# Attention's output projection per 256 rows by seven block products in place of eight

## The chip, the cores and the metric

The kernel runs on one core of a Trainium2 chip, in one launch. The core has a matrix engine (TensorE, PE in the profile, with its weight loads as PEld), three engines for work on elements (VectorE or DVE, ScalarE or ACT, GpSimd or POOL), and queues for transfers between DRAM and the on-chip memory (SBUF); matrix results land in eight banks of a second memory (PSUM). Each engine executes its own list in the order in which it was written down, and waits for the others through semaphores. The metric is the device time of one execution in microseconds (us): the median of some runs.

## The reference

One encoder layer is applied to two sequences of 1024 rows and 1024 columns, in fp32. Beside attention there is a Fourier mixing, which is not touched. What matters here:

```python
q = (rmsnorm(q_lat, g_q_lat) @ w_uq).reshape(b, s, MLA_HEADS, QK_DIM)      # 4 heads
...
p = jax.nn.softmax(sc, axis=-1)
o = einsum('bhqk,bkhd->bqhd', p, v)                                        # width 4 * 128 = 512
mix = jnp.concatenate([y_mla, y_four], axis=-1) @ w_out                    # the output projection
x = x + ga1 * mix                                                          # gate per sequence
h2 = rmsnorm(x, g_ffn) * (1.0 + sc2) + sh2
ffn = (silu(h2 @ w_gate) * (h2 @ w_up)) @ w_down
return x + ga2 * ffn
```

The kernel multiplies `w_out` with the values' up-projection ahead of time, so that each head's output is taken straight in the latent space of 128 columns: per sequence the attention half of the output projection is a product of (1024 rows x 512) with a (512 x 1024) matrix `wv`, which also carries the gate `ga1`.

## The kernel before

**Numbers.** Every fp32 product is made from pieces. A value is split into a high part, rounded to the type fp32r, and the rest (`split`, lines 62 to 64: a copy on ScalarE, a subtraction on VectorE), and `mm3` (lines 78 to 81) adds high x high, high x low and low x high in one bank. So each 128 x 512 piece of a product with 128 rows in the contraction is three matmuls, whose lines in the profile are 79, 80 and 81.

**Stages.** Input projections; the Fourier mixing (`p2`); attention (`p3`, with the output projection and the norm behind it, `p4`); the feed-forward (`p5`), which already works with seven products in place of eight on 512 x 512 blocks. The Fourier result and the input x are added in DRAM in `fo_d`; `out_load` fetches 128 of its rows into a tile `x2`, the output projection adds to it, `norm2` stores it, squares it and scales it, and `flip_h` transposes it for the feed-forward.

**Attention's loop.** Line 1499 runs k over 64 items, sequence s by block b of 256 rows by head h by half block u of 128 rows, and four steps more. Step k issues, in this order: `scores` of item k (10 matmuls, maximum on VectorE, exponential on ScalarE, scaling on VectorE), queries of the next block (`rope_q`, `rope_flip`, `absorb_q`), after each second head `values` of the pair (24 matmuls into one bank, j = 0 or 1), the transposes and splits of item k-1 (`flip_p`), then with m = k - 10 the output of the block that is a block and two steps behind (`out_step`), and what `todo[k]` has (weights, loads, additions of x). `out_proj` makes 128 rows x 512 columns of one block from 4 heads x 3 = 12 matmuls, in steps 0, 2, 4 and 6 of eight, in a bank of the pair `g`, which queries and `values` use too; one addition on VectorE takes it to `x2`. `wv` is loaded, gated on POOL (`wv_gate`) and split (`wv_split`) for sequence 0 in steps 5 to 13 and for sequence 1 in steps 37 to 43.

**Order.** A planner writes each engine's list: of what is ready by its own estimate of durations, what comes first in the program goes first. `tc.issue_after(x)` keeps instructions behind x on x's engine, `behind()` behind the last split, and `first(early, late)` keeps an order of two instructions. A tile with `bufs=n` has n buffers; a new one waits for the release of the one n before. Pools opened after others were closed use their bytes, and wait tile by tile.

**The seam.** Steps 64 to 67 issue `out_proj` of block (1,2), the last transposes and the last `values`. Then the pools of the feed-forward are opened. `prep_h` loads and splits seven prepared blocks `H` of sequence 0 (staging tiles H20, H21, H30, H31; two pieces for each `next(prep)`), `sums_w` makes the first weight combinations on VectorE, `out_proj` of block (1,3) follows in four pieces, with `norm3`, `flip2` (16 transposes of block (1,2)) and more of `prep_h` between; the feed-forward's weight chunk is split by `hl`. The first chunk (n = 0) uses one H per product and splits the others on the way; the second chunk's weight sums are made on VectorE in it.

## Time and profile before

| | |
|---|---|
| time, median of 3 runs | 1994.22 us (1994.19 to 1996.29) |
| the profiled execution | 1991.72 us, its span 1989.9 us |
| TensorE busy | 1965.3 us (99%), 9554 matmuls |
| VectorE, ScalarE, POOL busy | 1382.5 (69%), 893.7 (45%), 831.0 (42%) us |
| granted TensorE clock | 0.998 |
| attention, first scores to last | 278.3 to 682.0 us |
| matmuls of the output projection | 384, from 331.2 to 714.3 us |

The profile shows one execution, so its durations add up to its own time, 1991.72 us, which is 2.5 us below the median. Busy time of an engine is the time in which it executed anything; matmuls overlap each other, so the step from one start to the next is shorter than one duration.

### The profile page before, as it was taken

To read this page: it belongs to the slowest core of one execution; us is meant where nothing else is said; L and a number is where in the kernel's file an instruction comes from. 1 tells how busy PE (TensorE), PEld (TensorE's weight loads), DVE (VectorE), ACT (ScalarE), POOL (GpSimd) and SP (SyncE) were. 2 spreads that over 40 slices of the span, in tenths; PEclk is the share of its full clock that TensorE was granted. 3 is DMA by queue.
4 is the path that set the end of the run, shared out by engine and by line. 5 is a ranking of instruction groups with operands and counts; after the bars stand their busy time and mean duration, and the time that the engine had idled before them with its cause. 6 is when DMAs were issued, how large, how long until landed. Compare 5 with 4: busy or idle time off the path is not lost.

```text
span 1989.9 us, 27639 instructions
## 1 busy us (share of the span) xinstructions
PE 1965.3 (99%) x9554; PEld 1621.7 (81%) x9554; DVE 1382.5 (69%) x2081; ACT 893.7 (45%) x1743; POOL 831.0 (42%) x1008
## 2 busy tenths in 40 slices
PE   8999999999999999999999999999999999999998
PEld 6788778888888878888888888888888888888886
DVE  5667767666777687877767668779655665656794
ACT  5764545555565563333333355443333333335551
POOL 2554012111312348977877401345644544510152
PEclk9999999999999999999999999999999999999999
DMA  9986965535354584654655597774322322357762
GB/s 392 333 318 227 358 237 116 110 91 160 101 117 138 191 283 166 218 181 172 200 182 190 171 316 231 239 230 150 133 96 90 132 94 92 116 199 241 254 228 85
DMA packets 167081, 377.12 MB, mean 190 GB/s; under 512 B 18044, under 2 KB 43260, under 8 KB 163740
## 3 DMA queue, kind: packets, MB, share of 16 engines
q1 hardware_dynamic: 144252, 304.03, 45.2%
q0 software_dynamic: 22112, 70.27, 11.4%
q8 instruction: 75, 1.23, 0.2%
q10 hardware_dynamic: 576, 1.05, 0.1%
q14 instruction: 66, 0.54, 0.1%
HBM read 263.01 MB, written 120.65 MB: 193 GB/s over the span
## 4 chain that ended last, share of the span: by engine, by line
PE 59%; DVE 2%; issue 1%; POOL 1%; DMA 1%; ACT 0%; SPq 0%; POOLq 0%; DVEq 0%; ACTq 0%
PE bank L80 20%; PE bank L79 20%; PE bank L81 20%; DVE wl L64 1%; DMA draw<-in_w_down_dram 1%; DVE val L1987 0%; DVE val L154 0%; DVE val L1878 0%; DVE H L64 0%; DMA val<-x_d 0%; POOL rs_y L107 0%; POOL val L154 0%; DVE val L151 0%; POOL out_dram L1993 0%; DVE val L1875 0%
## 5 line engine op out<-in xcount | busy, mean ns | idle before, releaser
L79 PE MATMUL bank<-H,wh 128*128 128x512 f32 x1232 | 480.2, 390 | 2.6 <-DVE val L154 0.9
L80 PE MATMUL bank<-H,wh 128*128 128x512 f32 x1232 | 479.5, 389 | 0.3 <-DVE H L64 0.3
L81 PE MATMUL bank<-H,wl 128*128 128x512 f32 x1232 | 479.3, 389 | 0.2 <-DVE wl L64 0.2
L79 PEld LDWEIGHTS bank<-H,wh 128*128 128x128 f32 x1232 | 231.2, 188 | 53.2 <-DVE val L1861 2.0
L64 DVE TENSOR_TENSOR wl<-draw,wh 128x512 fp32r<-128x512 f32 x286 | 209.0, 768 | 94.0 <-ACT wh L63 93.5
L81 PEld LDWEIGHTS bank<-H,wl 128*128 128x128 f32 x1232 | 231.3, 188 | 49.0 <-DVE wl L64 0.5
L80 PEld LDWEIGHTS bank<-H,wh 128*128 128x128 f32 x1232 | 231.3, 188 | 48.2 <-DVE H L64 0.6
L154 DVE TENSOR_TENSOR val<-bank,val 128x512 f32<-128x512 f32 x200 | 136.6, 689 | 163.0 <-PE bank L81 162.1
L63 ACT CAST wh<-draw 128x512 fp32r<-128x512 f32 x286 | 164.9, 619 | 173.2 <-PE bank L80 131.6
L154 POOL TENSOR_TENSOR val<-val 128x512 f32<-128x512 f32 x58 | 82.4, 1421 | 345.7 <-DVE val L1959 163.5
L80 PE MATMUL bank<-wl,wh 128*128 128x512 f32 x572 | 223.2, 390 | 0.8 <-DVE wl L64 0.5
L63 ACT CAST wh<-rgu 128x512 fp32r<-128x512 f32 x172 | 107.1, 623 | 258.4 <-PE bank L80 203.2
L81 PE MATMUL bank<-wh,wl 128*128 128x512 f32 x572 | 222.6, 389 | 0.0
L79 PE MATMUL bank<-wh 128*128 128x512 f32 x572 | 222.6, 389 | 0.0
L63 ACT CAST wh<-val 128x512 fp32r<-128x512 f32 x133 | 82.3, 622 | 261.9 <-PE bank L80 249.3
L64 DVE TENSOR_TENSOR wl<-val,wh 128x512 fp32r<-128x512 f32 x133 | 126.1, 950 | 65.4 <-ACT wh L63 65.3
L64 DVE TENSOR_TENSOR wl<-rgu,wh 128x512 fp32r<-128x512 f32 x172 | 162.5, 945 | 0.8 <-ACT wh L63 0.7
L151 POOL TENSOR_TENSOR val<-rgu 128x512 f32<-128x512 f32 x80 | 108.3, 1354 | 78.7 <-DMA rgu<-in_wgu_dram 74.9
L80 PEld LDWEIGHTS bank<-wl,wh 128*128 128x128 f32 x572 | 107.4, 188 | 25.2 <-DVE wl L64 2.9
L79 PEld LDWEIGHTS bank<-wh 128*128 128x128 f32 x572 | 107.4, 188 | 22.5
L81 PEld LDWEIGHTS bank<-wh,wl 128*128 128x128 f32 x572 | 107.4, 188 | 21.9
L151 POOL TENSOR_TENSOR val<-val 128x512 f32<-128x512 f32 x89 | 119.1, 1356 | 1.3
(403 smaller groups left out, 3885.5 us busy)
## 6 DMA issues: line engine op xcount, KB each, us to landing
rgu<-in_wgu_dram SPq DMA_DIRECT2D x86, 512.0 KB, 4.0
draw<-s_d SPq DMA_DIRECT2D x143, 256.0 KB, 3.4
s_d<-val POOLq DMA_DIRECT2D x88, 256.0 KB, 3.0
draw<-t_d SPq DMA_DIRECT2D x88, 256.0 KB, 4.2
s_d<-val SPq DMA_DIRECT2D x66, 256.0 KB, 3.8
draw<-in_w_down_dram SPq DMA_DIRECT2D x55, 256.0 KB, 4.1
xt<-in_x_dram SPq DMA_DIRECT2D x16, 512.0 KB, 7.3
wada<-in_w_ada_dram SPq DMA_DIRECT2D x16, 512.0 KB, 9.8
```

The costliest lines, as they stand in the source:

```text
L63: here["a"] = nc.scalar.copy(hi, src).ins
L64: here["v"] = (eng or nc.vector).tensor_tensor(out=lo, in0=src, in1=rd(hi), op=ALU.subtract).ins
L79: nc.tensor.matmul(out, lh, rh, start=first, stop=False, skip_group_check=cont)
L80: nc.tensor.matmul(out, lh, rl, start=False, stop=False, skip_group_check=cont)
L81: here["t"] = here["pe"] = nc.tensor.matmul(out, ll, rh, start=False, stop=last, skip_group_check=cont).ins
L151: return eng.tensor_tensor(out=out, in0=x, in1=y, op=ALU.subtract).ins
L154: eng.tensor_tensor(out=out, in0=x, in1=y, op=ALU.add)
```

## The change

A block of 256 rows x 512 (the heads' outputs, transposed) times 512 x 1024 is cut in halves along all three axes: rows u, heads 0-1 and 2-3, columns g. Seven products of 128 rows x 256 x 512 columns, each 2 chunks x 3 matmuls, take the place of eight. With A the left operand and B the weights, they are m1 = A11 B11, m2 = A12 B21, m3 = S4 B22, m4 = A22 (B21 - T2), m5 = S1 T1, m6 = S2 T2, m7 = S3 (B22 - B12), where S1 = A21 + A22, S2 = S1 - A11, S3 = A11 - A21, S4 = A12 - S2, T1 = B12 - B11 and T2 = B22 - T1. The results are C11 = m1 + m2, C21 = m1 + m6 + m7 + m4, C22 = m1 + m6 + m7 + m5, C12 = m1 + m6 + m5 + m3.

The left operands are made when `values` is done, the weights once per sequence (`wv_sum` on POOL, seven products' weights split in `wv_split`). One product is issued per step, in the order of `PROD`; the sum m1 + m6 goes to three places by additions on POOL. Row half 1 is complete after m4, row half 0 after m3, so `norm2` and `flip_h` take them in that order. The first four products of block (1,2) are issued in steps 58 to 61 in place of after the loop. The tiles for this take 18 KB per partition more in `p4`; four tags get one buffer less each, H60 and H61 go to a pool that opens after `p4` is closed, and the row tile `x3` is dropped. The functions `sub` and `add` that are called are one tensor_tensor each on the engine named (lines 151 and 154).

```diff
     def half(name):
-        return e.tile([P, 512], F32, tag="hv", name=name, bufs=2)
+        return e.tile([P, 512], F32, tag="hv", name=name, bufs=1)
...
-        qp = e.tile([P, HEADS, P], F32R, tag="qp", name="qp", bufs=4)
+        qp = e.tile([P, HEADS, P], F32R, tag="qp", name="qp", bufs=3)
...
-        qa = [e.tile([P, 256], F32R, tag=f"qa{i}", name=f"qa{i}", bufs=3) for i in range(2)]
+        qa = [e.tile([P, 256], F32R, tag=f"qa{i}", name=f"qa{i}", bufs=2) for i in range(2)]
         split(qa[0], qa[1], pq[:, :256])
         S["qa", s, b, h] = qa
...
-    wv = [tl.tile([P, HEADS, D], F32R, tag=f"wv{i}", name=f"wv{i}") for i in range(2)]
+    wv = [tl.tile([P, 7, 2, 512], F32R, tag=f"wv{i}", name=f"wv{i}") for i in range(2)]
...
-    def out_proj(s, b, u, g):
-        o, x2 = S["o", s, b], S["x2", s, b, u]
-        us = slice(u * P, u * P + P)
-        gs = slice(512 * g, 512 * g + 512)
+    PROD = ("m1", "m7", "m6", "m5", "m4", "m2", "m3")
+    WEIGHT = {"m1": 0, "m2": 1, "m3": 2, "m5": 3, "m6": 4, "m7": 5, "m4": 6}
+
+    def part(name, bufs=1):
+        return [tl.tile([P, 2, P], F32R, tag=f"{name}{i}", name=f"{name}{i}", bufs=bufs) for i in range(2)]
+
+    def rest(name):
+        return tl.tile([P, 2, P], F32, tag=name, name=name, bufs=1)
+
+    def low(t, src, eng):
+        here["a"] = nc.scalar.copy(t[0], src).ins
+        eng.tensor_tensor(out=t[1], in0=src, in1=rd(t[0]), op=ALU.subtract)
+
+    def left_half(s, b, po):
+        f = S["f", s, b] = {"a21": rest("fa"), "s3": rest("fs")}
+        o = S["o", s, b] = {"m1": part("oa")}
+        nc.scalar.copy(f["a21"], po[:, :, 1, :])
+        split(*o["m1"], po[:, :, 0, :])
+        sub(f["s3"], po[:, :, 0, :], f["a21"], nc.vector)
+
+    def right_half(s, b, po):
+        f, o = S["f", s, b], S["o", s, b]
+        for k, u in (("m2", 0), ("m4", 1)):
+            o[k] = part(("ob", "oc")[u])
+            split(*o[k], po[:, :, u, :])
+        s2, s4 = rest("ft"), rest("fu")
+        sub(s2, po[:, :, 1, :], f["s3"], nc.vector)
+        add(f["a21"], f["a21"], po[:, :, 1, :], nc.vector)
+        sub(s4, po[:, :, 0, :], s2, nc.vector)
+        for k, v in (("m6", s2), ("m5", f["a21"]), ("m3", s4)):
+            o[k] = part(f"o{k}")
+            low(o[k], v, nc.gpsimd)
+
+    def out_proj(s, b, i):
+        k = PROD[i]
+        o, x = S["o", s, b], [S.get(("x2", s, b, u)) for u in range(2)]
+        lh, ll = o.pop(k)
+        wi = WEIGHT[k]
         pm = gbank()
-        for h in range(HEADS):
-            mm3(pm, o[0][:, h, us], o[1][:, h, us], wv[0][:, h, gs], wv[1][:, h, gs], h == 0, h == HEADS - 1)
-        here["v"] = nc.vector.tensor_tensor(out=x2[:, gs], in0=x2[:, gs], in1=pm, op=ALU.add).ins
+        for c in range(2):
+            mm3(pm, lh[:, c, :], ll[:, c, :], wv[0][:, wi, c, :], wv[1][:, wi, c, :], c == 0, c == 1)
+        if k == "m1":
+            S["u"] = tl.tile([P, 512], F32, tag="u", name="u", bufs=1)
+            nc.scalar.copy(S["u"], pm)
+            o["m7"] = part("oa")
+            low(o["m7"], S.pop(("f", s, b))["s3"], nc.gpsimd)
+
+        def to(u, g, v, eng=None):
+            t = x[u][:, 512 * g : 512 * g + 512]
+            here["v" if eng is None else "p"] = (eng or nc.vector).tensor_tensor(out=t, in0=t, in1=v, op=ALU.add).ins
+
+        for u, g in {"m1": ((0, 0),), "m7": ((1, 0), (1, 1)), "m5": ((1, 1), (0, 1)), "m4": ((1, 0),), "m2": ((0, 0),),
+                     "m3": ((0, 1),)}.get(k, ()):
+            to(u, g, pm)
+        if k == "m6":
+            here["v"] = nc.vector.tensor_tensor(out=S["u"], in0=S["u"], in1=pm, op=ALU.add).ins
+            for u, g in ((1, 0), (1, 1), (0, 1)):
+                to(u, g, S["u"], nc.gpsimd)
...
-        if i % 2 == 0:
-            out_proj(s, b, i // 4, i // 2 % 2)
-        if i in (2, 6):
-            norm2(s, b, i // 4, tl)
-        if i == 4:
-            flip_h(s, b, 0)
+        if i < 7:
+            out_proj(s, b, i)
+        if i in (4, 6):
+            norm2(s, b, 3 - i // 2, tl)
+        if i == 6:
+            flip_h(s, b, 1)
...
-            p = w.tile([P, N], F32, tag="p", name="p", bufs=3)
+            p = w.tile([P, N], F32, tag="p", name="p", bufs=2)
...
-            if j == 0:
-                S["o", s, b] = [tl.tile([P, HEADS, 256], F32R, tag=f"o{i}", name=f"o{i}b{s}{b}", bufs=3) for i in range(2)]
-            o = S["o", s, b]
             po = gbank()
             for c in range(8):
                 mm3(po, ckv[:, c, 0, :], ckv[:, c, 1, :], pth[:, c], ptl[:, c], c == 0, c == 7)
-            split(o[0][:, 2 * j : 2 * j + 2, :], o[1][:, 2 * j : 2 * j + 2, :], po.rearrange("p (h q) -> p h q", h=2))
+            (left_half, right_half)[j](s, b, po.rearrange("p (h u q) -> p h u q", h=2, u=2))
...
-        def wv_split(i):
-            h, g = i % 4, i // 4
-            gs = slice(512 * g, 512 * g + 512)
-            with behind():
-                split(wv[0][:, h, gs], wv[1][:, h, gs], S.pop(("wv", h, g)))
+        def wv_split(k, blk):
+            wi = WEIGHT[k]
+            for c in range(2):
+                with behind():
+                    split(wv[0][:, wi, c, :], wv[1][:, wi, c, :], S["wv", 2 * (blk // 2) + c, blk % 2])
+
+        def wv_sum(out, x, y):
+            for c in range(2):
+                o, x_, y_ = (S["wv", 2 * (blk // 2) + c, blk % 2] for blk in (out, x, y))
+                with tc.issue_after(here["p"]):
+                    here["p"] = sub(o, x_, y_, nc.gpsimd)
...
+        for q, k0 in enumerate((4, 36)):
+            for i in range(8):
+                todo[k0 + i // 4].append(lambda i=i: wv_gate(i))
+                if i == 3:
+                    todo[k0].append(lambda q=q: gate_half(q, 1))
+            for d, k, blk, sums in ((2, "m1", 0, ((0, 1, 0), (1, 3, 1))), (4, "m7", 1, ()), (4, "m3", 3, ((3, 3, 0),)),
+                                    (5, "m6", 3, ()), (6, "m5", 0, ()), (6, "m2", 2, ((2, 2, 3),)), (7, "m4", 2, ())):
+                todo[k0 + d].append(lambda k=k, blk=blk: wv_split(k, blk))
+                for out, x, y in sums:
+                    todo[k0 + d].append(lambda out=out, x=x, y=y: wv_sum(out, x, y))
...
-            todo[60 + u].append(lambda u=u: out_load(1, 2, u))
+            todo[57].append(lambda u=u: out_load(1, 2, u))
...
+                if k == nit:
+                    out_proj(1, 2, 4)
+                    norm2(1, 2, 1, tl)
+                    for i in (5, 6):
+                        out_proj(1, 2, i)
+                    S["tail", 3] = here["v"]
...
+            if 48 <= m < 52:
+                out_proj(1, 2, m - 48)
...
-            return w.tile([P, 4, 512], dt, tag=tag, name=tag, bufs=1)
+            return (S["w6"] if tag[:2] == "H6" else w).tile([P, 4, 512], dt, tag=tag, name=tag, bufs=1)
...
-                x2 = tl.tile([P, D], F32, tag="o0", name="x3", bufs=3) if u == 0 else xn
+                x2 = xn
...
-            first(here["a"], S.pop(("tail", 5)))
-            first(here["v"], S.pop(("tail", 6)))
-            first(here["v"], S.pop(("tail", 2)))
-            first(here["v"], S["tail", 4])
-            first(here["a"], S.pop(("tail", 7)))
...
-        norm2(1, 2, 1, xb)
+        norm2(1, 2, 0, xb)
...
-        for n in range(4):
-            out_proj(1, 3, n // 2, n % 2)
-            if n == 1:
-                norm3(0)()
-            prep_step((2, 0, 0, 0)[n])
-            if n == 1:
+        for n in range(7):
+            out_proj(1, 3, n)
+            if n == 4:
...
+        S["w6"] = st.enter_context(tc.tile_pool(name="p5c", bufs=1, reuse_waits="tile"))
+        for i in range(2):
+            quad(f"H6{i}")
...
-                            S["n3"] = norm3(1, S.pop("jk3").bitcast(BF16))
+                            S["n3"] = norm3(0, S.pop("jk3").bitcast(BF16))
```

28 lines of the change are left out of this document (8 added, 20 removed).

## The prediction

> **What bounds the kernel now.** I read the page's first part, then the groups of matmuls, then stretches of the span, and last the timeline where attention ends.
>
> ```profile
> span 1989.9 us, 27639 instructions
> ## 1 busy us (share of the span) xinstructions
> PE 1965.3 (99%) x9554; PEld 1621.7 (81%) x9554; DVE 1382.5 (69%) x2081; ACT 893.7 (45%) x1743; POOL 831.0 (42%) x1008
> ```
>
> TensorE (PE) is busy for 99% of the span, and only 24.6 us are without a matmul. Work that leaves TensorE shortens the kernel, unless another engine then sets the pace. The groups touched are these (instructions | busy, mean ns of one):
>
> ```profile
> L79 PE MATMUL gb<-wv,o0b 128*128 128x512 f32 x128 | 52.3, 408 | 0.0
> L81 PE MATMUL gb<-wv,o1b 128*128 128x512 f32 x128 | 51.0, 399 | 0.0
> L80 PE MATMUL gb<-wv,o0b 128*128 128x512 f32 x128 | 50.7, 396 | 0.0
> ```
>
> 384 matmuls belong to the output projection: 8 blocks of 256 rows, 4 pieces each, 12 matmuls a piece. Their 400 ns aren't the price, since matmuls overlap. The price is the step from start to start, read from the timeline of TensorE:
>
> ```profile
> 682.00 0.39 PE L1399 MATMUL ps_s<-lat,qp 128*128 128x512 f32 x1
> ...
> 689.70 0.39 PE L79 MATMUL gb<-pt,ckv 128*128 128x512 f32 x1
> ...
> 705.82 0.39 PE L81 MATMUL gb<-wv,o1b 128*128 128x512 f32 x1
> ...
> 714.55 0.39 PE L79 MATMUL bank<-H,wh 128*128 128x512 f32 x1
> ```
>
> From 689.70 to 705.82 TensorE starts 72 matmuls without a break (24 of the last `values`, 48 of `out_proj`): 16.12 us / 71 = 0.227 us each. The same rows give the landmarks of the seam: the last scores at 682.00, the last `values` from 689.70, the feed-forward's first product at 714.55. The stretches (length, then PE, PEld, DVE, ACT and POOL busy):
>
> ```profile
> 690.50:714.50 24.00, 23.18 (x110) 18.75 (x109) 15.46 (x20) 12.71 (x21) 7.78 (x21) 1.00 0.78 283
> 714.50:735.00 20.50, 18.37 (x84) 14.00 (x83) 20.30 (x26) 16.18 (x23) 8.15 (x9) 1.00 0.71 246
> 284.00:682.00 398.00, 395.28 (x2178) 333.74 (x2177) 285.94 (x526) 224.84 (x457) 96.84 (x154) 1.00 0.47 126
> ```
>
> In attention (284 to 682) TensorE lacks only 2.7 us of 398, and VectorE (DVE) is busy 72%: TensorE sets the pace. In the first 20.5 us of the feed-forward it is the other way round: VectorE is busy 20.30 of 20.50 us, TensorE 18.37. The chain that ended last says the same, for between these two pieces all its named work is VectorE's:
>
> ```profile
> 720.72 1.21 DVE wl L64 x2
> ...
> 735.01 0.50 PE bank L79
> ```
>
> **What the change removes.** A block has 7 products of 2 chunks x 3 matmuls = 42 matmuls instead of 48. Over 8 blocks that is 48 fewer, 48 x 0.227 = 10.9 us. That is the most the change can give. How much of it stays depends on where the matmuls go. Now six blocks (288 matmuls) lie ahead of 682.00 and 96 behind. The loop of the changed kernel issues the first four products of block (1,2) in steps 58 to 61, so 6 x 42 + 24 = 276 lie ahead and 60 behind. Ahead of the last scores 12 x 0.227 = **2.7 us** are saved; behind them TensorE has 36 x 0.227 = 8.2 us less to do.
>
> **What it adds.** The prices (groups of one stretch of attention, and one pair of steps of VectorE):
>
> ```profile
> L1343 DVE TENSOR_TENSOR x<-x,gb 128x512 f32<-128x512 f32 x18 | 12.2, 679 | 1.6 <-PE gb L81 1.6
> L1468 POOL TENSOR_TENSOR wvr<-wvr,gah 128x512 f32<-128x512 f32 x8 | 11.8, 1510 | 0.0
> ...
> L64 DVE TENSOR_TENSOR qa<-gb,qa 128x256 fp32r<-128x256 f32 x18 | 7.5, 416 | 0.6 <-ACT qa L63 0.6
> ...
> L64 DVE TENSOR_TENSOR o1b<-gb,o0b 128x512 fp32r<-128x512 f32 x9 | 6.2, 693 | 18.3 <-ACT o0b L63 18.3
> L1023 POOL TENSOR_TENSOR qt<-qt 128x256 f32<-128x256 f32 x8 | 5.9, 736 | 36.8 <-DVE qt L1022 36.8
> ...
> L63 ACT CAST qa<-gb 128x256 fp32r<-128x256 f32 x18 | 6.7, 372 | 17.0 <-PE gb L81 17.0
> ```
>
> ```profile
> 713.93 1.51 DVE L1343 TENSOR_TENSOR xn<-xn,gb 128x512 f32<-128x512 f32 x2
> 715.35 0.69 DVE L64 TENSOR_TENSOR wl<-rgu,wh 128x512 fp32r<-128x512 f32 x1
> 715.96 0.69 DVE L64 TENSOR_TENSOR wl<-H,wh 128x512 fp32r<-128x512 f32 x1
> ```
>
> Instructions of VectorE overlap a little: 0.69 us of duration is a step of 0.61 us (715.35 to 715.96), so I count 0.61 for 512 columns and, with the same 0.08 off, 0.34 for 256.
>
> Per block, VectorE: `left_half` has two 256-column operations and `right_half` five, in place of two 512-column splits: 7 x 0.34 - 2 x 0.61 = +1.2. The products bring nine 512-column additions instead of four: +3.1. Together **+4.3 us** of VectorE per block. ScalarE: eight operations of 256 columns (0.37 each) and one copy of 512, instead of two casts of 512, +2.4 us. GpSimd (POOL): four subtractions of 256 columns (0.74) and three additions of 512 (1.4 to 1.5), so 7.3 us per block where it had none. Per sequence the weights take 14 splits instead of 8 (6 x 0.61 = 3.7 us more on VectorE) and 8 new subtractions on POOL (8 x 1.4 = 11 us). DMAs: no bytes are added; `out_load` of (1,2) moves up by three steps on SP's queue, ahead of the feed-forward's loads there, and its 512 KB transfers now share time with scores, which read no DRAM. That I cost at nothing; without that cover it would delay the loads behind it by their own issue, under 1 us. At nothing too: the rows of block (1,3) now load into the two slots X2 and X3 (both behind the last scores, 8 us ahead of the first addition that needs them), the two buffers H60 and H61 move to a pool that opens when `wv` is done (the fourth product needs them 8 us after the first), and the order of the two row halves in `norm2` and `flip_h` is turned round.
>
> **In attention.** A block lasts 398 / 63 x 8 = 50.5 us now (63 steps between 284 and 682), and 49.1 with six matmuls fewer. VectorE needs 285.94 / 398 x 50.5 = 36.3 us of it, and 40.6 after: 83%. In the two blocks where weights are prepared it is 44.3, 90%. It should keep up, but it executes in order and it has waits of its own, of which this one can't move, since the softmax must wait for its exponential (who waited for whom, us in total, 284 to 690):
>
> ```profile
> DVE rr L1410 <- ACT p L1409: 26.3, 42, 1.4
> ```
>
> That is 3.3 us a block, so the two weight blocks stand at 47.6 of 49.1 us. The two psum banks that products, queries and values share are held longer too: `right_half` reads its bank five times with VectorE, and the product m5 adds twice, behind POOL's three additions of m6 (4.3 us). I take **+2 us** for stalls of TensorE here, the size of what it already has there (2.7 us). Bounds: 0, if VectorE's slack swallows all, and +8, if each weight block loses 4 us. The smaller buffer counts (`p` 3 to 2, `qp` 4 to 3, `hv` 2 to 1, `qa` 3 to 2) I cost at nothing: a buffer is rewritten a step (6.3 us) or more after TensorE has read it in program order. If that cover is gone, scores wait for transposes, up to 1.0 us a step.
>
> **In the seam.** The last `values` can't start earlier after the last scores than now (682.00 to 689.70 is maximum, exponential, scaling, transposes and splits of the last row block). TensorE has 18 matmuls of (1,2) and the 16 transposes to fill that, instead of 24 and 16; the gap of 1.4 us costs nothing more, as the chain of the softmax runs either way. So the start of the seam moves by 2.7 us only. Behind it TensorE needs 24.0 - 30 x 0.227 = 17.2 us up to the feed-forward (42 matmuls of block (1,3) instead of 72). VectorE needs the 15.46 it has there, plus 5 x 0.34 - 0.61 = 1.1 for `right_half`, plus three additions more (1.8): 18.4 us. **VectorE becomes the bound**, where it was idle for 8.5 us. The stretch behind it is already VectorE's: its 20.30 lose one addition, 19.7. Together 18.4 + 19.7 = 38.1 us at best, against 44.5 now: -6.4. I do not take that whole, because VectorE waits at fixed places: for the `values` product, for POOL's three additions and its chain for the norm, and for the second H, whose staging tile H21 now lies on the bytes of `ckv` and can be loaded only when the last `values` is done (the first two KB of `ckv`, counted from the tile sizes in the pool's order). The row for such a wait is this:
>
> ```profile
> 713.26 0.75 DVE L1640 TENSOR_SCALAR xn<-x,rs_r 128x1024 f32<-128x1024 f32 x1 [3.35 <-POOL rs_r L111]
> ```
>
> I take one wait of that kind and round down, 2.9 us: the seam gives **-3.5 us**. Bounds: -6.4 with no wait, and +1 if the 8.5 us of waits all stay (38.1 + 8.5 = 46.6, less about 1 us that overlaps, against 44.5).
>
> **The sum.** -2.7 - 3.5 + 2 = -4.2 us. The profiled execution took 1991.72 us (span 1989.9), so 1987.5 there; it was 2.5 us under the median 1994.22, and against that median I forecast **1990.0 us**. Most of the 10.9 us is lost at a place where TensorE isn't the bound.
>
> **One rule against the change.** GpSimd's work lengthens some of VectorE's:
>
> ```profile
> L1411 DVE TENSOR_SCALAR p<-p,rr x64: 745/754/1591, 284.6 to 686.0; 128x1024 f32<-128x1024 f32 x64
> ```
>
> The scaling of p takes 0.754 us in the median and 1.591 at most; the long ones fall while POOL works. [...]
>
> **Rivals.**
>
> First, *the whole gain*: the seam fills its waits and attention loses nothing. -2.7 - 6.4 = -9.1, up to the full -10.9: about 1984. For it: VectorE has 28% free in attention; the order of each engine is planned anew, and products that are ready can be put ahead. Against it: 20.30 of 20.50 us in the stretch from 714.50.
>
> Second, *VectorE becomes the bound in attention, through POOL*: slower. Place: the ten operations of a block that work from SBUF in the fast form (eight scalings of p, two of the norm). If POOL's 7.3 us more meets all ten, VectorE needs 40.6 + 10 x 0.84 + 3.3 = 52.3 us a block against 50.5 now: 8 x 1.8 = 14, plus 2 x 3.7 for the weight blocks, less 3.5 in the seam: +18, 2012 us. It decides from 49.1 - 40.6 - 3.3 = 5.2 us a block, six of ten operations met, and is slower than before from about seven. For it: POOL goes from 24% (96.84 of 398) to about 40% busy. Against it: at 24% the median is still the short form. A milder form, with only the weight blocks saturated, is 2000 us.
>
> Third, *no gain*: the seam's waits all stay, -2.7 + 1 + 2 = about 0: 1994 us. For it: xn, rstd and the loads are chains of latency that no missing matmul shortens. Against it: several hang on TensorE's own additions, which come earlier.
>
> **Chances.** Forecast 0.46 (its own range 1986.5 to 1993), whole gain 0.18, slower through POOL 0.18, no gain 0.18. Differences under 0.2%, 4 us, can't be told from none in this kernel. A little more than half of the forecast's own range lies beyond -4 us: faster 0.18 + 0.27 = 0.45; within 0.19 + 0.18 = 0.37; slower 0.18. The range reaches from the whole gain with a small loss to the milder form of the second rival: 1984.5 to 1999.
>
> **What will show it.** Right: 336 matmuls of `gb<-wv` at a step of 0.227; VectorE at 80 to 85% in attention with TensorE's idle time there at 4 to 5 us; in the seam VectorE over 90% busy from the start of the last `values` on, and that stretch to the second weight chunk at about 41 us. Wrong: TensorE idle over 10 us in attention, or the mean of the scaling of p near 1.3 us (second rival); waits of VectorE for POOL or DMA of 8 us in the seam (third); TensorE busy without a gap there (first). The sum would also fail if the slower start of the feed-forward's weights, whose tiles lie on `wv` and wait for the last product, costs more than the 1 us it has now.

## The result, and the profile after

| | before | after |
|---|---|---|
| time, median | 1994.2 us (1991.45 to 1996.29) | 2017.88 us (2017.33 to 2019.68) |
| ratio | | 1.0121, interval 1.0104 to 1.0139 |
| profiled execution, its span | 1991.72, 1989.9 us | 2017.47, 2014.9 us |

The change makes the kernel slower by 1.2%, some 24 us, where I had forecast 4 us less, and the time lies outside the range. The first part of the page after (busy us, share of the span, number of instructions):

```profile
span 2014.9 us, 27891 instructions
## 1 busy us (share of the span) xinstructions
PE 1966.2 (98%) x9506; PEld 1618.5 (80%) x9506; DVE 1430.3 (71%) x2173; ACT 915.8 (45%) x1811; POOL 913.3 (45%) x1080
```

The 48 matmuls are gone (9554 - 9506), as the arithmetic says, and yet TensorE is busy for just as long as before (1965.3 us) and idle for 48.7 us in place of 24.6. Both halves of that need an explanation: the idle time, and matmuls that got dearer. The landmarks, from TensorE's timeline after (start, duration, in brackets the idle time ahead of it and who ended it):

```profile
691.80 0.39 PE L1449 MATMUL ps_s<-lat,qp 128*128 128x512 f32 x1
...
698.51 0.49 PE L79 MATMUL gb<-pt,ckv 128*128 128x512 f32 x1
...
701.06 0.50 PE L80 MATMUL gb<-pt,ckv 128*128 128x512 f32 x1 [2.05 <-DVE pt L64]
...
711.03 0.47 PE L79 MATMUL gb<-wv,oa 128*128 128x512 f32 x1 [2.87 <-DVE fu L151]
...
718.75 0.77 PE L79 MATMUL gb<-wv,oa 128*128 128x512 f32 x1 [5.62 <-DVE xn L1385]
719.32 0.63 PE L80 MATMUL gb<-wv,oa 128*128 128x512 f32 x1
719.74 0.63 PE L81 MATMUL gb<-wv,oa 128*128 128x512 f32 x1
...
737.56 0.50 PE L79 MATMUL bank<-H,wh 128*128 128x512 f32 x1 [0.71 <-ACT wh L63]
...
762.28 0.50 PE L79 MATMUL bank<-H,wh 128*128 128x512 f32 x1 [0.49 <-DVE val L154]
```

| landmark | before | after | later by |
|---|---|---|---|
| last scores | 682.00 | 691.80 | 9.8 |
| last values | 689.70 | 698.51 | 8.8 |
| feed-forward's first product | 714.55 | 737.56 | 23.0 |
| 93 matmuls further on (77 of the feed-forward, 16 transposes) | 737.45 | 762.28 | 24.8 |
| end of the span | 1989.9 | 2014.9 | 25.0 |

So 9.8 us are lost up to the last scores, 13.2 in the seam from there to the feed-forward (45.76 us long in place of 32.55), 1.8 in the feed-forward's first 93 matmuls (24.72 in place of 22.89), and 0.2 after them. Below I call the first three parts attention, seam and first chunk. (The product at 735.01 with which the prediction ends its first chunk comes ten matmuls sooner than the one at 762.28, so those two don't compare.) Windows after (length, then PE, PEld, DVE, ACT and POOL busy, the granted clock, DMA share, GB/s):

```profile
284.00:691.80 407.80, 397.30 (x2169) 334.21 (x2169) 327.18 (x610) 244.12 (x519) 168.13 (x219) 0.99 0.46 122
520.00:577.00 57.00, 50.87 (x280) 41.78 (x278) 52.52 (x90) 37.88 (x81) 35.41 (x40) 1.00 0.47 113
691.80:737.56 45.76, 30.40 (x118) 22.47 (x116) 26.25 (x40) 20.16 (x37) 15.47 (x28) 0.81 0.58 207
710.00:720.00 10.00, 3.35 (x9) 2.28 (x10) 7.52 (x11) 4.08 (x8) 3.36 (x4) 0.60 1.02 368
737.56:762.28 24.72, 22.07 (x93) 17.01 (x94) 23.75 (x30) 19.41 (x30) 12.11 (x12) 0.93 0.70 241
```

and the three of before that answer to the second, third and last (a count can include a matmul that runs across an edge):

```profile
520.00:577.00 57.00, 56.86 (x316) 47.92 (x316) 44.16 (x79) 34.61 (x72) 14.11 (x24) 1.00 0.48 116
682.00:714.55 32.55, 31.73 (x154) 25.65 (x153) 22.05 (x31) 17.61 (x30) 7.78 (x21) 1.00 0.75 274
714.55:737.44 22.89, 20.75 (x94) 15.97 (x93) 22.68 (x30) 18.62 (x28) 9.52 (x10) 1.00 0.74 257
```

**Attention**, counted from 284 us, is 407.80 us long in place of 398.00: -2.7 for the 12 matmuls fewer, as forecast; +7.8 of idle time (10.50 us against 2.72 before); +0.5 because the first scores already start 0.5 us later in this profile (278.79 against 278.32); and the rest, +4.2, for matmuls that keep TensorE busy for longer (397.30 us against 395.28, with 12 fewer). Of that, 2.7 lie from 339.85 to 346.86, behind waits of 1.55, 0.46 and 1.21 us at 337.83, 339.27 and 342.98: eight transposes take 1.91 us there (1.03 at 348.71) and seven matmuls step by 0.42 to 0.43, at a granted clock of 0.79 from 334 to 344 and 0.86 from 344 to 354. Where it happens is read from the maxima of the softmax on VectorE, one for each item, here items 37 and 46, before and then after, with the splits of weights and scalings of p between them:

```profile
511.69 1.23 DVE L1404 TENSOR_REDUCE mx<-ps_s 128x1 f32<-128x1024 f32 x1 [0.88 <-PE ps_s L1399]
...
575.99 1.22 DVE L1404 TENSOR_REDUCE mx<-ps_s 128x1 f32<-128x1024 f32 x1 [0.66 <-PE ps_s L1399]
```

```profile
513.02 1.22 DVE L1454 TENSOR_REDUCE mx<-ps_s 128x1 f32<-128x1024 f32 x1
...
527.33 1.87 DVE L1461 TENSOR_SCALAR p<-p,rr 128x1024 f32<-128x1024 f32 x1
529.72 2.87 DVE L64 TENSOR_TENSOR wv<-wvr,wv 128x512 fp32r<-128x512 f32 x2
...
537.38 1.72 DVE L1461 TENSOR_SCALAR p<-p,rr 128x1024 f32<-128x1024 f32 x1
...
584.66 1.23 DVE L1454 TENSOR_REDUCE mx<-ps_s 128x1 f32<-128x1024 f32 x1
```

TensorE's longest wait in that stretch is for one of these scalings:

```profile
539.25 1.06 PE L1474 MATMUL ppt<-ident,p 128*128 128x128 f32 x8 [2.80 <-DVE p L1461]
```

The delay is 1.33 us at item 37, 8.67 at item 46, nine items on: that is the second weight stretch. The first (315 to 362 us) does the same, +6.5. Between the two, the new kernel is *faster* than the old by some 1.5 us a block, where the six matmuls that each block lost are worth 1.4. At the last item, whose scores now have 24 matmuls of block (1,2) ahead of them, the delay is 9.8. In the stretch from 520 to 577 VectorE is busy 52.52 of 57 us (92%) where it was 44.16, and TensorE lacks 6.1 us where it lacked 0.14. The scaling of p takes 1.87 and 1.72 us in it (before, over all items, 0.754 in the median and 1.591 at most), and a pair of weight splits 2.87 (a pair of the same shape takes 1.28 at 700.32 below), with POOL busy 35.41 of the 57 us.

**The seam** has 8.2 us less of matmuls, 14.5 us more without any (15.36 idle against 0.82), and 6.9 because the matmuls that are left take longer (30.40 us busy against 31.73, with 8.2 less to do; the granted clock is 0.81 against 1.00). VectorE is *not* full there: 26.25 of 45.76 us. What it waits for, and in which order, is in its timeline after:

```profile
700.32 1.28 DVE L64 TENSOR_TENSOR pt<-ppt,pt 128x512 fp32r<-128x512 f32 x2
...
708.60 0.42 DVE L64 TENSOR_TENSOR ob<-gb,ob 128x256 fp32r<-128x256 f32 x1 [7.00 <-ACT ob L63]
...
712.30 1.63 DVE L64 TENSOR_TENSOR H<-H,H 128x1024 fp32r<-128x1024 f32 x1 [1.42 <-ACT H L63]
...
717.93 0.68 DVE L1385 TENSOR_TENSOR xn<-xn,gb 128x512 f32<-128x512 f32 x1
...
719.13 0.68 DVE L1385 TENSOR_TENSOR x<-x,gb 128x512 f32<-128x512 f32 x1
```

and in that of before:

```profile
690.56 2.35 DVE L64 TENSOR_TENSOR H<-H,H 128x1024 fp32r<-128x1024 f32 x2
...
695.98 0.69 DVE L64 TENSOR_TENSOR o1b<-gb,o0b 128x512 fp32r<-128x512 f32 x1 [3.07 <-ACT o0b L63]
```

Before, VectorE split the feed-forward's first H while TensorE made the last values, and had only the rest of that time to wait (3.07 us). After, it stands idle for 7.00 us at the head of `right_half`, and the first H, which TensorE needs last of all, comes *behind* that, at 712.30. Behind H in turn stand the additions that free the two g banks: the one at 719.13 belongs to the last product of block (1,2), whose matmuls ended ahead of 698.51, so its bank was held for 20 us. With one bank left, TensorE waits 5.62 us, up to 718.75, for the addition at 717.93 to free it.

A smaller wait of this kind comes ahead of the last values: at 699.65 VectorE waits 1.33 us for POOL's `rs_r` to scale a row block, the last splits of p's transposes (700.32) stand behind that, and TensorE has its 2.05 us at 701.06. The change, e9 and e12 to e16 all have this wait on VectorE, 1.33 to 1.93 us long.

**The first chunk** is VectorE's, as it was (23.75 of 24.72 us, 96%; 22.68 of 22.89 before), and now 1.8 us longer.

### The profile page after: what moved, and what is told of

Read it like the earlier page. It is cut to its first block, busy times and chain, and to the rows that moved or that the text cites. A ratio compares the mean times of both kernels' runs of the same rounds, so it can differ in the third digit from the quotient of the medians.

```text
span 2014.9 us, 27891 instructions
## 1 busy us (share of the span) xinstructions
PE 1966.2 (98%) x9506; PEld 1618.5 (80%) x9506; DVE 1430.3 (71%) x2173; ACT 915.8 (45%) x1811; POOL 913.3 (45%) x1080
## 3 DMA queue, kind: packets, MB, share of 16 engines
q8 instruction: 74, 1.21, 0.2%
## 4 chain that ended last, share of the span: by engine, by line
PE 81%; DVE 6%; DMA 4%; POOL 3%; issue 3%; ACT 1%; POOLq 0%; DVEq 0%; ACTq 0%; SPq 0%
PE bank L80 21%; PE bank L79 21%; PE bank L81 21%; PE gb L79 3%; PE gb L80 3%; PE gb L81 3%; PE ppt L1474 2%; DMA wada<-in_w_ada_dram 2%; PE ps_s L1447 1%; DMA val<-x_d 1%; PE ps_s L1448 1%; PE ps_s L1449 1%; PE ps_s L1445 1%; PE ps_s L1446 1%; DVE wl L64 1%
## 5 line engine op out<-in xcount | busy, mean ns | idle before, releaser
L80 PEld LDWEIGHTS bank<-H,wh 128*128 128x128 f32 x1232 | 231.8, 188 | 49.1 <-DVE H L64 1.2
```

Of the source, the lines that this page charges most:

```text
L80: nc.tensor.matmul(out, lh, rl, start=False, stop=False, skip_group_check=cont)
```

## The experiments

A landmark in the table below is from each run's own profile; seam is the time from the last scores to the feed-forward's first product. The first scores start between 278.1 and 280.7 us in these profiles, so differences of one or two us between the last scores are not read; the seam is a difference within one profile. Ratios are against the kernel before, run beside it.

| run | median us | ratio (interval) | last scores | seam |
|---|---|---|---|---|
| before | 1994.2 | 1 | 682.00 | 32.55 |
| after | 2017.88 | 1.0121 (1.0104, 1.0139) | 691.80 | 45.76 |
| e1_free_add | 2019.3 | 1.0129 (1.0113, 1.0144) | 691.18 | 42.6 |
| e2_spread | 2027.39 | 1.0162 (1.0145, 1.0179) | 699.27 | 46.22 |
| e3_no_sums | 2016.49 | 1.0115 (1.0097, 1.0132) | 686.39 | 47.9 |
| e4_single_buffers | 1995.65 | 1.0005 (0.9995, 1.0014) | 683.79 | 32.58 |
| e5_eight_splits | 2011.58 | 1.0078 (1.0061, 1.0095) | 685.40 | 44.0 |
| e6_cover_behind | 2018.6 | 1.0111 (1.0096, 1.0126) | 691.87 | 44.35 |
| e7_more_weight_work | 2005.95 | 1.0051 (1.0036, 1.0066) | 694.45 | 32.55 |
| e8_three_highs | 2009.39 | 1.0069 (1.0054, 1.0084) | 692.44 | 37.11 |
| e9_old_order | 2013.64 | 1.0096 (1.0081, 1.0111) | 690.80 | 42.30 |
| e10_old_order_staging | 2015.13 | 1.0101 (1.0086, 1.0116) | 693.91 | 42.19 |
| e11_free_order | 2021.05 | 1.013 (1.0115, 1.0145) | 693.65 | 49.31 |
| e12_one_weight_a_step | 2019.75 | 1.0124 (1.0107, 1.0141) | 693.09 | 45.82 |
| e13_cover_and_order | 2016.48 | 1.0112 (1.0096, 1.0129) | 691.38 | 44.12 |
| e14_seam_in_order | 2020.33 | 1.0126 (1.0111, 1.0141) | 693.04 | 45.88 |
| e15_kept_busy | 2017.45 | 1.0115 (1.0099, 1.0132) | 691.36 | 45.66 |
| e16_order_no_cover | 2010.99 | 1.008 (1.0065, 1.0095) | 692.25 | 39.43 |
| e17_both_causes | 2004.27 | 1.0047 (1.003, 1.0063) | 685.33 | 34.57 |

### What the smaller buffers cost

**e4_single_buffers**, the kernel before with the four smaller tags alone (the lines cut to tag and count):

```diff
-hv bufs=2, qp bufs=4, qa bufs=3, p bufs=3
+hv bufs=1, qp bufs=3, qa bufs=2, p bufs=2
```

> The kernel before with the smaller buffer counts alone (p 3 to 2, qp 4 to 3, hv 2 to 1, qa 3 to 2). Theory A (the buffers cost nothing, as predicted): 1994 us, within 2 us. Rival B (they tie the engines closer and are part of the loss in attention): 1997 to 2003 us.

1995.65 against 1995.21 us beside it, ratio 1.0005: nothing, as I had costed it. That is for the kernel before; whether the smaller buffers cost something in the fuller stretches of the changed one, no run tests.

### Attention: the weights

**e3_no_sums**, the change with the POOL subtractions of `wv_sum` left out:

```diff
-                    todo[k0 + d].append(lambda out=out, x=x, y=y: wv_sum(out, x, y))
+                    pass
```

> The changed kernel without the 16 subtractions that combine the weights on POOL; the products then use uncombined weights, so this part of the computation is left out. Theory A (POOL's work lengthens VectorE's operations from SBUF in the weight stretches): the mean of the scalings of p in these stretches falls from about 1.4 us towards 1.1, and the time falls by 4 to 8 us. Rival B (the six more splits per sequence and the banks make the loss): falls by under 2 us.

The last scores come 5.4 us earlier (686.39). The total hardly moves: the seam is 2.1 us longer (47.9), and another 2 us go behind it. What attention gives, later parts can take back. (This kernel leaves the combination of the weights out.)

**e5_eight_splits**, without the differences and with four of the seven weights split (the other products read the split ones, so the combination is left out here too):

```diff
-    WEIGHT = {"m1": 0, "m2": 1, "m3": 2, "m5": 3, "m6": 4, "m7": 5, "m4": 6}
+    WEIGHT = {"m1": 5, "m2": 1, "m3": 2, "m5": 4, "m6": 4, "m7": 5, "m4": 1}
...
-                todo[k0 + d].append(lambda k=k, blk=blk: wv_split(k, blk))
+                if k in ("m7", "m3", "m6", "m2"):
+                    todo[k0 + d].append(lambda k=k, blk=blk: wv_split(k, blk))
...
-                    todo[k0 + d].append(lambda out=out, x=x, y=y: wv_sum(out, x, y))
+                    pass
```

> The changed kernel with as much weight work on VectorE and GpSimd as the kernel before had: no differences of weights, and only four of the seven weights are split (eight splits a sequence instead of fourteen); the products m1, m4 and m5 read another product's weight, so the combination of the weights is left out of the computation. In the changed kernel the two stretches in which the weights are made cost 6.5 and 7.5 us. Theory W (the added weight work is what costs them): the last scores start 12 to 14 us sooner than in the changed kernel (691.8), near 679, and if the seam is as long as there the time is 2004 to 2008 us. Theory P (what a block of seven products itself puts on VectorE, GpSimd and the two banks leaves no room for any weight work): leaving the differences out gave 5.4 us there, and six splits fewer add under 2 us: last scores at 685 or later, time 2012 or more.

The last scores come 6.4 us earlier and the median falls by 6.3. Its window of the second weight stretch:

```profile
520.00:577.00 57.00, 53.51 (x283) 44.59 (x282) 44.93 (x85) 35.52 (x77) 21.51 (x31) 0.97 0.46 113
```

VectorE is back at 44.93 us, where it was before the change (44.16), from 52.52; TensorE lacks 3.5 us in place of 6.1, but before the change it lacked 0.14. So VectorE's busy time alone doesn't set the stall. Most of the 3.5 is one wait, with an idle VectorE ahead of it:

```profile
528.81 0.76 DVE L1403 TENSOR_SCALAR xn<-x,rs_r 128x1024 f32<-128x1024 f32 x1 [2.36 <-POOL rs_r L111]
```

```profile
532.22 1.07 PE L1474 MATMUL ppt<-ident,p 128*128 128x128 f32 x8 [2.45 <-DVE p L1461]
```

The scaling of a row block stands ahead of the scaling of p in VectorE's list and waits for POOL, and TensorE waits for p. The last scores came at 685.40, where I had put the theory that the blocks' own work leaves no room; the other one said 679.

**e7_more_weight_work**, the other way round: the kernel before, with its eight products, given the six more splits and eight more POOL operations per sequence, doing nothing useful (weights are changed and changed back):

```diff
+            x, y = S["wv", i % 4 - 1, i // 4], S["wv", i % 4, i // 4]
+            for op in (ALU.subtract, ALU.add):
+                with tc.issue_after(here["p"]):
+                    here["p"] = nc.gpsimd.tensor_tensor(out=x, in0=x, in1=y, op=op).ins
...
+            if i not in (0, 4):
+                todo[39 + i // 2 + i // 4].append(lambda i=i: wv_split(i))
+                todo[6 + i // 2 + 2 * (i // 4)].append(lambda i=i: wv_split(i))
```

> The kernel before, with the weight work of the changed one added to it: in each sequence six of the eight splits are made twice, and GpSimd makes eight more additions and subtractions of 128x512 on the raw weights (each pair gives the weight back). Theory W: last scores 12 to 14 us later than before's 682.0, at 694 to 696, time 2006 to 2009 us. Theory P: with eight products a block there is room for it: under 4 us, last scores 682 to 686, time 1994 to 1998.

The last scores move from 682.00 to 694.45, +12.45 us, with the seam unchanged at 32.55. Attention began 0.7 us later in this profile, so 11.8 are for the weights' extra work alone. That is the size of what the change lost in attention beside my 2.7 us (12.0, counted the same way), though not split in the same way over the two stretches (about +9.2 and +2.5 here, +6.5 and +7.3 there), so the agreement of the two sums is in part chance.

**e2_spread** and **e12_one_weight_a_step** spread the same splits, one weight a step in place of two, the first kernel over steps 2 to 8 and the second over steps 3 to 9 (the two added lines, in this order; both tables cut to step and weight):

```diff
-((2, "m1"), (4, "m7"), (4, "m3"), (5, "m6"), (6, "m5"), (6, "m2"), (7, "m4"))
+((2, "m1"), (3, "m7"), (4, "m3"), (5, "m6"), (6, "m5"), (7, "m2"), (8, "m4"))
+((3, "m1"), (4, "m7"), (5, "m3"), (6, "m6"), (7, "m5"), (8, "m2"), (9, "m4"))
```

> The changed kernel with the weights' splits at one product a step (steps 2, 3, 4, 5, 6, 7, 8 after the start) instead of two products in two of the steps. Theory A (VectorE is overfull in the weight stretches only because the splits are bunched): each of the two stretches loses 2 to 3 us instead of 6 to 7, the time falls by 6 to 10 us. Rival B (it is the sum of the work and POOL's hold on VectorE, not the bunching): falls by 0 to 3 us.

> The changed kernel with the seven weights split one a step, at steps 3 to 9 of each stretch (the run with steps 2 to 8 was 9.5 us slower than the changed kernel: there the split of the second weight stood at step 3, behind GpSimd's last gates). Theory G (a split that stands ahead of GpSimd's gates and differences in VectorE's order stops VectorE, and with it TensorE): one step later they no longer wait, last scores 3 to 7 us sooner than 691.8, time 2011 to 2015 us. Theory F (VectorE is full in the stretches, wherever the splits stand): last scores within 2 us of 691.8, time 2016 to 2020.

Neither helps: the last scores at 699.27 and 693.09 in place of 691.80. In the second stretch, e2 and then e12:

```profile
520.00:577.00 57.00, 48.52 (x256) 40.09 (x255) 45.79 (x75) 34.39 (x74) 31.90 (x38) 0.94 0.34 82
```

```profile
520.00:577.00 57.00, 51.78 (x282) 42.82 (x281) 45.35 (x85) 36.89 (x79) 29.93 (x38) 0.97 0.39 89
```

So the bunching isn't the cause. VectorE is not full there either: it is busy for 80% of these 57 us, and TensorE lacks 8.5 and 5.2. As in e5, what VectorE waits for with p behind it counts as well as how much it does.

### The seam: order, cover, clock

**e1_free_add** takes away the hint that keeps the last addition of block (1,2) behind the first weight combinations:

```diff
-            first(here["s"], S["tail", 3])
```

> The changed kernel with one order hint taken out: the last addition of block (1,2), product m3, is no longer kept behind the feed-forward's first weight sums. Theory A (held bank): in the changed kernel m3's matmuls end at 697.2 us, but its addition comes at 719.13 us, so one of the two banks g is held for 22 us and TensorE goes through the seam with one bank. Then, with the hint gone, the last scores to the feed-forward's first product take 26 to 32 us instead of 45.5, no wait of TensorE over 3 us is left there, and the time falls from 2017.9 by 13 to 18 us, to 2000 to 2005. Rival B (VectorE has too much to do in the seam, whatever the order): the wait for the bank goes over into waits for VectorE's other work, and the time falls by 0 to 4 us only.

The seam is 3.2 us shorter, and the total isn't. VectorE and TensorE a little later:

```profile
737.95 0.75 DVE L1696 TENSOR_SCALAR xn<-xn,rs_r 128x1024 f32<-128x1024 f32 x1 [2.92 <-DMA x_d<-xn]
```

```profile
745.17 0.80 PE L80 MATMUL bank<-H,wh 128*128 128x512 f32 x1 [3.90 <-DVE H L64]
```

Now the norm of x3 heads VectorE's list. It is made in place, since the change dropped the tile x3, so it waits for the store of the same rows; the splits of H stand behind it and TensorE waits 3.90 us for them.

**e6_cover_behind** puts the products m2 and m3 of (1,2) back behind the last values:

```diff
                     norm2(1, 2, 1, tl)
+                if k == nit + 2:
                     for i in (5, 6):
                         out_proj(1, 2, i)
```

> The changed kernel with the last two products of block (1,2) issued behind the last values product, as the kernel before has two of its four there. Theory C (the seam is long because nothing covers the making of the left operands): the values product ends 2.7 us sooner, one product covers half of the 2.9 us wait for the operands, the feed-forward starts 1.5 to 4 us sooner than 737.6, time 2013 to 2016 us. Theory V (VectorE's order is what holds the banks: feed-forward splits and sums stand ahead of the additions that free them): within 1 us of the changed kernel's 2017.9.

The seam is 1.4 us shorter, and the total isn't (2018.6).

**e9_old_order** gives back two of the five hints which the diff dropped, so that the first H is split ahead of `right_half` on ScalarE and VectorE:

```diff
+            S.setdefault(("rh", s, b), (here["a"], here["v"]))
...
+            for i, late in zip("av", S["rh", 1, 3]):
+                first(here[i], late)
```

> The changed kernel with two of the five order hints that the change took out put back in their sense: the first two splits of feed-forward operands stand ahead of the splits of block (1,3)'s second values product, on ScalarE and on VectorE, where the kernel before has them. In the changed kernel VectorE is idle for 7.0 us ahead of those splits and makes the two operands behind them, ahead of the additions that free the banks. Theory V (VectorE's order behind the last values product is the seam's bound): the 2.4 us and their waits leave the path, the feed-forward starts 2 to 5 us sooner than 737.6, time 2013 to 2016 us. Theory C (the chain of operands, banks and GpSimd's additions): under 1 us, time 2017 or more.

```profile
700.51 2.35 DVE L64 TENSOR_TENSOR H<-H,H 128x1024 fp32r<-128x1024 f32 x2
...
707.62 0.42 DVE L64 TENSOR_TENSOR ob<-gb,ob 128x256 fp32r<-128x256 f32 x1 [4.76 <-ACT ob L63]
```

The H split fills a part of the wait (4.76 us left of 7.00), the seam is 3.5 us shorter and the median 4.2 lower: two lines of order are worth as much as all I had forecast for the change.

**e10_old_order_staging** takes, besides, the staging tile H21 off the bytes of `ckv` (a tag changes its place):

```diff
-("ckv", 2048, 1), ("ql0", 512, 2), ("ql1", 512, 2), ("rc", 512, 1), ("rs", 512, 1)
+("rc", 512, 1), ("ckv", 2048, 1), ("ql0", 512, 2), ("ql1", 512, 2), ("rs", 512, 1)
```

> The run before this one, with the table of rc put ahead of ckv in memory, so that the staging tile H21 no longer lies on ckv: its loads are issued near 693 instead of 708.2, where the values product has ended. If the late load holds the second feed-forward operand and that the feed-forward: 1 to 3 us sooner than the run with the two hints alone. If the splits stand too late in VectorE's order anyhow: within 1 us of it.

The load that I had named is indeed late in the change, and is early here (SP's queue, after and then this run):

```profile
708.19 0.88 SPq L1637 DMA_DIRECT2D H<-hc_d  x2
```

```profile
695.80 0.97 SPq L1638 DMA_DIRECT2D H<-hc_d  x2
```

Twelve us earlier, and the seam is 42.19 in place of 42.30. That wait was real and cost nothing.

**e11_free_order** is e10 without e1's hint:

```diff
-            first(here["s"], S["tail", 3])
```

> The run with the two hints and the moved staging tile, and the hint taken out that keeps the addition of (1,2)'s last product behind the sums of feed-forward weights (it holds a bank for 22 us in the changed kernel). Theory V: with the first splits out of the way and the bank free, the feed-forward starts 7 to 11 us sooner than 737.6 (leaving three operands' low halves out gave 8.0), time 2007 to 2011 us. Theory C: the bank's release gives the 3.8 us that taking this hint out alone gave, and the time stays at 2013 or more.

```profile
713.77 1.19 DVE L1404 TENSOR_SCALAR xn<-x,rs_r 128x1024 f32<-128x1024 f32 x1 [9.73 <-POOL rs_r L111]
```

49.31 us: with the hint gone the planner put the scaling of (1,2)'s rows ahead of H and of `right_half` on VectorE, where it waited 9.73 us for its rstd. An order that is left free is filled by estimates, and here by a wrong one.

**e13_cover_and_order** joins e6 and e9 (their two diffs).

> The two changes to the seam that each helped, together: the hints that put the first two feed-forward splits into VectorE's idle stretch (alone: the feed-forward 42.3 us after the last scores, against 45.8 in the changed kernel), and the last two products of (1,2) behind the last values product (alone: 44.4 us). If they are two causes, they add: 40.5 to 41.5 us after the last scores, time 2011 to 2013.5 us. If both only move the same wait: 42 us or more, time 2013.5 to 2016.

```profile
706.67 0.69 DVE L1386 TENSOR_TENSOR x<-x,gb 128x512 f32<-128x512 f32 x1 [5.50 <-PE gb L81]
```

44.12 us, worse than e9 alone: the products put behind the values have an addition on VectorE, which then stands at the head of its list and waits 5.50 us for them, with H (707.28) behind it.

**e14_seam_in_order** and **e16_order_no_cover** write the whole order of the seam by hand: H0 and the sums of weights ahead of `right_half`, H5 behind the additions of (1,3)'s first three products, the third H at product 4 in place of product 1, the 16 transposes behind m6. e14 has the cover of e6 too (the last lines of the diff), e16 has not:

```diff
-        with tc.issue_after(S.pop(("tail", 4))):
+            for i, late in zip("av", S["rh", 1, 3]):
+                first(here[i], late)
+        S.pop(("tail", 4))
+        with tc.issue_after(here["v"]):
...
+            first(here["s"], S["rh", 1, 3][1])
...
+            if n < 3:
+                for late in S["h5"]:
+                    first(here["v"], late)
...
-            prep_step((0, 2, 0, 0, 0, 0, 0)[n])
+            prep_step((0, 0, 0, 0, 2, 0, 0)[n])
...
+                if k == nit + 2:
                     for i in (5, 6):
                         out_proj(1, 2, i)
```

> As the run before this one, and VectorE's whole order in the seam set by hints, nothing left out: the sums of the feed-forward weights ahead of the splits of the last values product, the second feed-forward operand behind the additions of (1,3)'s first three products, the third behind its fifth product. Theory V (the place of feed-forward work in VectorE's and ScalarE's order, not its amount, made the seam long): the feed-forward starts 33 to 37 us after the last scores (45.8 in the changed kernel, 37.1 where three operands' low halves were left out), time 2005 to 2010 us. If the amount is what counts: what is moved behind the products comes back as waits of the feed-forward's first products, and the time stays above 2011.

> As the run with VectorE's whole order set, but with the last two products of (1,2) left where the changed kernel has them, ahead of the last values product. In that run the addition of the first of them stood at the head of VectorE's order and its last matmul came behind the values product, so VectorE was idle for 5.3 us and the feed-forward work set behind it ran in front of the splits after all. Here nothing at the head waits: the two splits and the sums (2.4 and 2.8 us) fit into the idle 7.0 us. Theory V (the order counts): the feed-forward starts 34 to 38 us after the last scores (42.3 with the two hints alone), time 2007 to 2011 us. Theory A (the amount counts): the waits move to the feed-forward's first products or to GpSimd's additions, 40 us or more, time 2012 or more.

VectorE in e14:

```profile
708.18 0.69 DVE L1386 TENSOR_TENSOR x<-x,gb 128x512 f32<-128x512 f32 x1 [5.34 <-PE gb L81]
708.79 2.35 DVE L64 TENSOR_TENSOR H<-H,H 128x1024 fp32r<-128x1024 f32 x2
...
713.84 0.42 DVE L64 TENSOR_TENSOR ob<-gb,ob 128x256 fp32r<-128x256 f32 x1
```

and in e16:

```profile
701.97 2.35 DVE L64 TENSOR_TENSOR H<-H,H 128x1024 fp32r<-128x1024 f32 x2
...
709.08 0.42 DVE L64 TENSOR_TENSOR ob<-gb,ob 128x256 fp32r<-128x256 f32 x1 [1.38 <-ACT ob L63]
```

In e14 one addition heads the list, waits 5.34 us for a product that was put behind the values, and H, sums and `right_half` stand behind it: `right_half` starts 4.0 us later than in e16, counted from the last scores. e14's seam, 45.88 us, is no shorter than the changed kernel's, against an expectation of 33 to 37. Without the cover the same order fills the wait (1.38 us left of 7.00), the seam is 39.43 us, 6.3 less, and the median 2010.99. My expectation for e16 of a seam that lets the feed-forward start 34 to 38 us behind the last scores was missed by 1.4 us.

**e8_three_highs** asks how much VectorE's H splits weigh at all: no low parts for the first three H.

```diff
+                bare = s == 0 and i < 3
+                H[k] = [quad(f"H{k}0", F32R)] * 2 if bare else [quad(f"H{k}{j}", F32R) for j in range(2)]
```

> The changed kernel without the low halves of the first three feed-forward operands (six subtractions of 128x1024 on VectorE; the products read the high half in their place, so this part of the computation is left out). Theory V: these six stand between the additions that free the two banks; without them the feed-forward starts 6 us or more sooner than 737.6, time 2009 to 2012 us. Theory C, or any other chain (the making of the left operands, GpSimd's three additions): under 2 us sooner, time 2015.5 or more.

The seam falls by 8.65 us, to 37.11, for six instructions of about 1.2 us each, 7 us: TensorE's idle time in it falls by 6.0 us, to 9.32, and the rest is quicker matmuls (clock 0.91). So the splits stand ahead of what TensorE waits for. (This kernel leaves the low parts out of the computation.)

**e15_kept_busy** fills the two long waits of TensorE in the seam with 12 and 22 matmuls whose results nobody reads, so that TensorE is busy there:

```diff
+        def keep_busy(n):
+            t = xp.tile([P, 512], F32, tag="d", name="db")
+            for _ in range(n):
+                ins = nc.tensor.matmul(t, wv[0][:, 0, 0, :P], wv[0][:, 0, 0, :], start=True, stop=True).ins
...
+                keep_busy((12, 22)[n])
```

> The changed kernel with 34 added matmuls of 512 columns into a bank that nothing reads, in TensorE's two longest waits of the seam (12 behind the last values product, 22 behind (1,3)'s first product), so that TensorE is busy there. In the changed kernel the matmuls behind these waits step by 0.43 us instead of 0.227 for some 3 us. If the clock falls because TensorE stood idle, the matmuls of m1 and m7 step by 0.227 here and the feed-forward starts 1 to 3 us sooner than 737.6, time 2015 to 2017 us; if the clock falls for another reason, they still step by 0.43 and the time is the changed kernel's 2017.9 or more.

```profile
710.00:720.00 10.00, 9.06 (x40) 6.87 (x39) 7.47 (x11) 4.58 (x8) 4.31 (x5) 1.00 1.00 367
```

In this window the clock stays at 1.00 where it had been 0.60, and the first five products of (1,3) step by 0.23 again. The seam: 45.66 in place of 45.76 us. So behind these two waits the slow matmuls are a consequence in this order of the lists: with quick ones TensorE waits longer for other engines. That covers a part of the 6.9 us only: the values product ahead of them and the product m2 behind them still have steps of 0.43, and the clock is 0.83 from 700 to 710 and from 730 to 740.

### Both causes together

**e17_both_causes** is e16 with the reduced weights of e5 (so the combination of the weights is left out).

> The run before this one, with the weight work in the attention as small as in the run with eight splits (no differences, four of seven weights split, so the combination of the weights is left out of the computation; 6.3 us faster than the changed kernel there). If the two stretches and the seam are separate causes, the gains add: 5.5 to 7 us less than the run before this one. If they hide one another, under 4 us. Whether it then reaches the kernel before (1995) tells whether anything else is lost: the products saved are worth 7 x 1.36 us in the attention and 2.7 us in the seam.

2004.27 us, 6.7 less than e16, where 5.5 to 7 were expected if the two causes add. Its seam and first chunk:

```profile
685.33:719.90 34.57, 25.60 (x118) 18.63 (x116) 27.21 (x39) 19.94 (x37) 15.88 (x27) 1.00 0.73 253
719.90:747.28 27.38, 22.10 (x93) 16.89 (x93) 24.88 (x30) 20.28 (x31) 15.20 (x14) 0.94 0.74 260
```

The total fits, its parts less so. Against e16 the last scores come 6.9 us earlier, about what the weights gave in e5 (6.4). But the seam is 4.9 us shorter too, though nothing in it was changed, and 5.1 are lost again: 2.7 in the first chunk, which takes e16 24.65 us for the same 93 matmuls, and 2.4 behind it. The 4.9 are slow matmuls: the seam's 118 keep TensorE busy for 25.60 us at a clock of 1.00 here and for 30.73 at 0.83 in e16 (its window is shown at the end of this document), with 8.97 and 8.70 us idle. So the attention's cause adds to the seam's, and that the sum came out so well is in part luck.

Against the kernel before, 9.4 us in the median are left; in the profiles it is 3.3 in attention, 2.0 in the seam, 4.5 in the first chunk (27.38 us for the 93 matmuls that took 22.89) and 1.8 behind it. The first chunk has as many VectorE instructions as after (30, 24.88 us) and is longer; TensorE's three longest waits in it, 1.96, 1.70 and 1.58 us, are for VectorE, and what makes VectorE later I did not take apart. No kernel with seven products was faster than the one before.

## Why the prediction was wrong

**The step on the weight stretches, "It should keep up", failed.** The term was +2 us with bounds 0 to +8; the runs give +12 (7.8 idle, 4.2 slower steps). The amount was nearly right: VectorE is busy 327.18 of 407.80 us, 80%, as forecast, and 92% in the second weight stretch, where I had worked out 90% and 47.6 us of 49.1 with the wait for the exponential. With 1.5 us of room in a block, I should have put the stall term at the upper bound, which would still have been short; instead I took the size of what was there before. The sum lacked two things that an amount of work doesn't show. Operations lengthen: the two scalings of p that lie wholly beside POOL's 128 x 512 operations took 1.72 and 1.87 us in that stretch, and those with none of these beside them 0.74 to 0.75. And VectorE waits with TensorE's next operand behind it: in e5, with nearly the old amount of work in the second stretch, 2.36 us for one scaling, and TensorE 2.45 us behind that. e7 shows that the weights' extra work alone, with the old products, costs 11.8 us; e5 that taking it away gives back 6.4. Between 6 and 12 the two don't agree, so how much belongs to the weights and how much to the blocks' own operations, when both stand together, stays open.

**The seam term, -3.5, failed by more: with the first chunk it is +15.0** (13.2 + 1.8), and its upper bound was +1. I had it as amounts of work: VectorE 18.4 + 19.7 us, "VectorE becomes the bound". In the seam it is busy 54% of the time from the last values on, by this window after:

```profile
698.51:737.56 39.05, 23.76 (x82) 17.50 (x82) 20.94 (x30) 15.92 (x28) 14.16 (x26) 0.78 0.55 197
```

The mark I had set, over 90%, fell. What I left out is the order of VectorE's list: the diff drops five `first` hints beside its arithmetic, and I read past them. I counted what each engine has to do and not what stands at the head of its list while it waits. e9 gives 3.5 us back with two of the hints, e16 6.3 with the order written out; e8, without six of the H splits, 8.65. Of the 13.2 in the seam, e16 leaves 6.9 and e17 2.0; between these two lie the 4.9 us of slow matmuls, for which the sum had no term, since it took every step at 0.227. The last 2.0 are not resolved: in e17 TensorE still stands idle for 8.97 us of the seam, so the 8.2 us of matmuls removed there have turned into waits.

**Smaller points.** Right: 336 matmuls in place of 384 (48 fewer on the page) and the -2.7 us ahead of the last scores, seen as some 1.5 us a block between the weight stretches; the smaller buffers at nothing (e4, in the old kernel); that the first chunk is VectorE's. Wrong by a little: the gap ahead of the last values was to cost nothing more. It is shorter up to their first matmul (6.71 us from the last scores, 7.70 before), but the second one then waits 2.05 us. Wrong in effect: the late load of H21, which is there and worth 0.1 us (e10). From the start of the last values to the product that was at 735.01 I forecast about 41 us, and it was 45.3 before; the same number of matmuls into the feed-forward it is now 759.34 - 698.51 = 60.8.

**The rivals.** The whole gain and no gain are out. Of the second, slower through POOL, the place and direction were right in its milder form, where only the weight blocks are saturated, and its sign of over 10 us of idle time in attention was met (10.50); the strong form was not right. The mean of the scaling of p, after and before:

```profile
L1461 DVE TENSOR_SCALAR p<-p,rr 128x1024 f32<-128x1024 f32 x64 | 57.3, 895 | 1.3
```

```profile
L1411 DVE TENSOR_SCALAR p<-p,rr 128x1024 f32<-128x1024 f32 x64 | 52.2, 816 | 1.5
```

It is 0.9 us and not near 1.3. The 0.84 us of this rival is the step from the median to the longest of these scalings before (0.754 to 1.591); the norm's scaling goes from 0.754 to 1.768 there (L1353, 14 of them, five at 1.75 or more). That all ten operations of a block would meet POOL's work was my estimate, and no run shows it: after, 16 of the 64 scalings of p take 1.00 us or more. That 2012 us of this rival lies near the 2017.88 measured is chance: it had -3.5 for the seam. None of my cases had a seam that gets longer by its order.
